# Softmax normalisation in a hybrid attention block: one reciprocal for four heads, normalising as a separate step

## The chip, the cores and the metric

The kernel runs on one core of one Trainium2 chip. The metric is the time of one execution on the device in microseconds (us). Engines: TensorE (PE; its weight loads are shown apart, as PEld), VectorE (DVE), ScalarE (ACT), GpSimd (POOL) and SyncE (SP), whose queue issues the loads from device memory.

## What is computed

One layer of a decoder block over 512 tokens of width 1024, in float32. Cut to what matters here (`masked_softmax` is an ordinary softmax over the allowed keys):

```python
h = rms_norm(x, norm_pre)
proj = h @ w_in                       # 15 pieces: queries, keys, values, gates, ...
kc, vc = compress_blocks(k_c, ...), compress_blocks(v_c, ...)   # flat @ w1, gelu, @ w2
# attention: 8 heads in 2 groups of 4; per head three branches with their own gates g
o = g[..., 0:1] * o_cmp + g[..., 1:2] * o_sel + g[..., 2:3] * o_win
y_a = (o * silu(z_n)) @ w_nsa_o
o_b = retention_sequence(q_r, k_r, v_r)        # chunks of 128 tokens, 4 heads
y_b = (group_norm(o_b) * silu(z_r)) @ w_ret_o
x = x + rms_norm((sigmoid(m_a) * y_a + sigmoid(m_b) * y_b) @ w_out, norm_post)
```

With 512 tokens all 8 key blocks are selected and the window covers the sequence, so the selected and the window branch are both causal softmax attention over all earlier tokens, with different keys and values.

## The kernel before

Every matrix product is done in three passes: each operand is split into a high half that TensorE takes in one pass and the low half that is left (`hi`, `lo`), and the product is hi x hi + lo x hi + hi x lo (`mm3`, lines 237 to 240). The weights stream through four buffers `raw` (512 KB a load, SP's queue, line 324). `cp_any` casts half of a load to `whi`, mostly on ACT (line 197), sometimes on DVE (line 205); `sub_split` makes `wlo` on DVE (line 209). There are nine pairs `whi`/`wlo` of 512 columns, and a new load is issued when a split has used up an old one (`split_lo`, lines 363 to 370).

The main sequence of PE (`main`, line 1202) goes through weight blocks: keys and values (A, C), queries (Q), two hidden layers of the compression (H0, H1: 256 columns wide, so each weight half serves two short products only), then Z, MA0, ZR0, QK0, VR0, ZR1, QK1, VR1, MB0, the two output projections and `w_out`. Each block's results go through PSUM; the banks `bank0` and `bank1` take turns as accumulators (`ACC`), so a block's next column of results can start only when the tail step of the one before last has read its bank.

Attention is woven between the blocks' products. A unit is one query tile t of 128 tokens (t = 3 first), one group of 4 heads, and one branch (t = 2, 3: L = 512 or 384 keys) or both branches together (t = 0, 1); there are 12 units. In a unit `att_head` (lines 787 to 821) runs for each of the four heads j:

- two score products into a bank (lines 793, 794),
- on DVE the masked row minimum of the negated scores, which also writes the negated scores to the probability tile P (line 802; it shows as a custom instruction and a read of its accumulator),
- on ACT exp with the row's sum z (line 809),
- on DVE one reciprocal of z, one column or two (line 811),
- the normalisation with 1/z and the branch's gate: one DVE instruction a branch (line 820), or, where the planner's clocks say that ACT is free sooner (line 813), a product 1/z x gate on DVE and a scaling on ACT (lines 814 to 817).

`att_unit` (line 870) waits for the four heads and starts `att_blocks` for pairs of key tiles: four transposes each on PE (line 831), then `att_half` copies them (ACT, high half; DVE, low half) and multiplies with the values. There are eight probability tiles P (`PR`); the last pair of key tiles by number gives a unit's four back (lines 833 to 835).

Nothing of this is written in the order in which it runs. Each step is a Python generator, and `Order.run` (line 90) is a planner: it holds estimated clocks of PE, ACT, DVE, POOL and the loads, adds an estimated cost for each instruction (lines 65 to 88, 187 to 235), and lets that step go on next whose inputs it holds to be ready, by rank. A step that would be too early (`LAG`, `MARGIN`, `SLACK`) waits. So a change in one step moves the instructions of others. The engines take their instructions in the planned order, and semaphores keep them correct where the estimates are off.

The retention (`tail_qk`, `ret`) shares the engines from block QK0 on; `rtab` is its rotary table, one buffer, loaded again for each tile (`load_rtab`, line 931).

Of the kernel before, what the change touches and what calls it, by code (L numbers as in the profile page):

```python
# [145 lines left out]
def block_kernel(ctx: ExitStack, tc, x, xT, g_pre, ws, small, w2s, norm_post, rope_r, dmask, out):  # L146
# [640 lines left out]
    def att_head(t, g, brs, j, slot):  # L787

        L, nb, h, b0 = P * (t + 1), len(brs), g * 4 + j, brs[0]
        s = yield from PS.get()  # L790
        sv = s[:, 0:nb * L].rearrange("p (b c) -> p b c", b=nb)
        q = qT[t][:, h, :]
        mm(sv, q, kA[:, b0:b0 + nb, g, 0:L], True, False)
        e = mm(sv, q, kB[:, b0:b0 + nb, g, 0:L], False, True)
        yield e, "dve"

        Pj = slot["P"]
        pv = Pj[:, 0:nb * L].rearrange("p (b c) -> p b c", b=nb)
        stat = sp.tile([P, 6], FT, name="stat", tag="stat", bufs=12)
        nm, z, rz = (stat[:, 2 * i:2 * i + 2] for i in range(3))  # L800
        for b in range(nb):
            V.tensor_tensor_reduce(pv[:, b, :], sv[:, b, :], maskp[:, 512 - L:512], 1.0, -NEG, OP.add, OP.min,  # L802
                                   nm[:, b:b + 1])
            od.op("dve", 1.04 * L + 80, e)
        e = od.op("dve", 80)
        PS.put(s, e)
        yield e, "act"
        for b in range(nb):
            e = act(pv[:, b, :], pv[:, b, :], AF.Exp, r=e, bias=nm[:, b:b + 1], scale=-1.0, accum_out=z[:, b:b + 1])
        yield e, "dve"  # L810
        e = recip(rz[:, 0:nb], z[:, 0:nb], e)
        gc = h * 3 + 1 + b0
        if max(od.eng["act"], e) + (0.833 * L + 186) * nb + 190 < max(od.eng["dve"], e) + (0.521 * L + 191) * nb:
            e = tt(rz[:, 0:nb], rz[:, 0:nb], gate[:, t, gc:gc + nb], OP.mult, e)
            yield e, "act"
            for b in range(nb):
                e = act(pv[:, b, :], pv[:, b, :], r=e, scale=rz[:, b:b + 1])
        else:
            for b in range(nb):
                e = ts(pv[:, b, :], pv[:, b, :], rz[:, b:b + 1], gate[:, t, gc + b:gc + b + 1], OP.mult, OP.mult, e)  # L820
        slot["pv"], slot["r"] = pv, e

    def att_blocks(t, g, todo, slots, lastblk):

        r = max(s["r"] for s in slots)
        yield lambda: "po" in avs[t, g]
# [2 lines left out]
        for (br, b, kt), pt in zip(todo, pts):  # L829
            for j in range(4):  # L830
                e = tr(pt[:, j * P:(j + 1) * P], slots[j]["pv"][:, b, kt * P:(kt + 1) * P], ident, r)
            od.spawn(att_half(t, g, br, kt, pt, e), 2)
        if lastblk:
            for s in slots:
                PR.put(s["P"], e)

# [14 lines left out]
    def attention():  # L851
        for t in reversed(range(NT)):
# [7 lines left out]
            for g in range(2):  # L860
                for brs in ([(0, 1)] if t <= 1 else [(0,), (1,)]):
                    slots = []
                    for j in range(4):
                        s = {"P": (yield from PR.get())}
                        slots.append(s)
                        od.spawn(att_head(t, g, brs, j, s), 3)
                        yield
                    od.spawn(att_unit(t, g, brs, slots), 2)

    def att_unit(t, g, brs, slots):  # L870
        yield lambda: all("r" in s for s in slots)
        todo = [(br, b, kt) for b, br in enumerate(brs) for kt in range(t + 1)]
        for i in range(0, len(todo), 2):
            od.spawn(att_blocks(t, g, todo[i:i + 2], slots, i + 2 >= len(todo)), 2)

    def att_out():
        for t, g in ((t, g) for t in reversed(range(NT)) for g in range(2)):
# [52 lines left out]

    def load_rtab(i, r):
        rtr[0] = od.dma(P * 2048, r)
        DMA.dma_start(rtab, rope_r[i // 4, i % 4 * P:(i % 4 + 1) * P, :])

    def tail_qk(hp, t, ps, e):
        yield od.need("q0", "q1", "q2", "q3", "cmp0", "cmp1", *([f"ret{hp - 1}{t}"] if hp else []))
        tv = rtab.rearrange("p (s a c) -> p s a c", s=2, a=4)
        pv = ps.rearrange("p (a r c) -> p a r c", a=4, r=2)
        t1 = yield from NAT.get()
# [457 lines left out]
```

## Time and profile before

| | us |
|---|---|
| median of 3 timed runs | 529.1 (529.02 to 531.55) |
| profiled execution | 532.1, of which span 530.3 |
| PE busy in the span | 519.5 |
| PEld (weight loads) busy | 437.1 |
| DVE busy | 383.2 |
| ACT busy | 253.8 |
| POOL busy | 13.6 |

The profiled execution's own time is 1.8 us longer than its span and 3.0 us above the median. A matmul's shown end is modelled and overlaps the next one's start, so PE can look busy for a short time in which it waits; the weight load in front of a matmul (PEld) starts after the wait, and what ended its idle time names the engine that was late. A row names the line of a helper for many operations (L197 for every ACT instruction, L209 for every two-input DVE operation), so the tiles tell them apart: `whi`, `wlo` are weights, `arena_f<-arena_f,stat` is a probability tile, `arena_r<-bank` the copy of transposed data.

### The profile page before, as it was taken

The numbers are of one execution on the slowest core, as the hardware profiler recorded it, in microseconds if no ns is written. First come the engines' busy times: TensorE is split into PE (matmuls) and PEld (weight loads), VectorE is DVE, ScalarE is ACT, GpSimd is POOL, SyncE is SP. The second block draws the span as 40 slices with busy tenths as digits, with TensorE's granted clock in tenths as the row PEclk, the third lists the DMA queues.
The fourth block names the chain that finished last, engine by engine and source line by source line (L and its number), as shares of the span: only waits on it lengthen the run. The fifth ranks groups of instructions, "written<-read, shape, count | busy, mean of one in ns | idle before, by whom it ended". The sixth has DMA issues, their size and how long they took to land.

```text
span 530.3 us, 7276 instructions
## 1 busy us (share of the span) xinstructions
PE 519.5 (98%) x2616; PEld 437.1 (82%) x2616; DVE 383.2 (72%) x920; ACT 253.8 (48%) x549; POOL 13.6 (3%) x32
## 2 busy tenths in 40 slices
PE   8999999999999999999999999999999999999995
PEld 7898887688888888888788888888888888888885
DVE  6779799988898889998867886786737235345533
ACT  6674577746465673755646253524304224113411
POOL 2000000000000000000010000000000000000000
PEclk9999999999999999999999999999999999999999
DMA  8932025602203014150501442131815043304022
GB/s 324 383 122 80 22 80 185 212 1 65 96 21 105 35 41 138 26 192 3 178 2 41 138 129 70 41 119 41 303 55 158 10 150 122 117 1 158 1 97 102
DMA packets 18131, 55.18 MB, mean 104 GB/s; under 512 B 2096, under 2 KB 3120, under 8 KB 18096
## 3 DMA queue, kind: packets, MB, share of 16 engines
q1 hardware_dynamic: 17808, 54.46, 30.6%
q8 instruction: 20, 0.33, 0.3%
q10 hardware_dynamic: 288, 0.27, 0.1%
q14 instruction: 15, 0.12, 0.1%
HBM read 52.63 MB, written 2.10 MB: 103 GB/s over the span
## 4 chain that ended last, share of the span: by engine, by line
PE 91%; DVE 4%; DMA 2%; issue 1%; ACT 1%; DVEq 0%; POOLq 0%; POOL 0%; ACTq 0%
PE bank L230 85%; PE bank L234 6%; DMA raw<-in_stream_dram 2%; DVE wlo L209 1%; ACT whi L197 1%; DVE arena_f L209 0%; DVE arena_r L209 0%; DVE arena_f L222 0%; DVE arena_f L218 0%; DVE nat L209 0%; DVE arena_r L222 0%; ACT arena_f L197 0%; DVE arena_f L802 0%; ACT arena_r L197 0%; POOLq L1393 0%
## 5 line engine op out<-in xcount | busy, mean ns | idle before, releaser
L197 ACT ACTIVATE whi<-raw 128x512 fp32r<-128x512 f32 x150 | 90.6, 627 | 53.9 <-PE bank L230 42.9
L209 DVE TENSOR_TENSOR wlo<-raw,whi 128x512 fp32r<-128x512 f32 x160 | 103.1, 686 | 6.6 <-ACT whi L197 5.9
L230 PE MATMUL bank<-whi,hTh 128*128 128x512 f32 x256 | 100.6, 409 | 1.6 <-DVE arena_r L222 1.1
L230 PE MATMUL bank<-wlo,hTh 128*128 128x512 f32 x256 | 97.1, 395 | 0.1
L230 PE MATMUL bank<-whi,hTl 128*128 128x512 f32 x256 | 97.1, 395 | 0.0
L230 PE MATMUL bank<-arena_r 128*128 128x256 f32 (+2 forms) x328 | 71.2, 336 | 0.1
L197 ACT ACTIVATE arena_r<-bank 128x512 fp32r<-128x512 f32 (+2 forms) x76 | 42.4, 572 | 48.6 <-PE bank L234 46.4
L230 PE MATMUL bank<-hTh,whi 128*128 128x512 f32 x160 | 64.2, 401 | 0.9 <-ACT whi L197 0.9
L230 PE MATMUL bank<-hTh,wlo 128*128 128x512 f32 x160 | 62.8, 392 | 0.1
L230 PE MATMUL bank<-hTl,whi 128*128 128x512 f32 x160 | 62.5, 391 | 0.0
L230 PE MATMUL bank<-arena_r,whi 128*128 128x512 f32 x192 | 59.1, 389 | 0.0
L230 PEld LDWEIGHTS bank<-whi,hTh 128*128 128x128 f32 x256 | 48.6, 190 | 11.0 <-DVE arena_r L222 1.5
L230 PEld LDWEIGHTS bank<-whi,hTl 128*128 128x128 f32 x256 | 48.6, 190 | 10.7
L230 PEld LDWEIGHTS bank<-arena_r 128*128 128x128 f32 x328 | 51.0, 189 | 6.7 <-DVE stat L802 0.4
L230 PEld LDWEIGHTS bank<-wlo,hTh 128*128 128x128 f32 x256 | 48.8, 191 | 9.0 <-DVE wlo L209 0.5
L209 DVE TENSOR_TENSOR arena_r<-bank,arena_r 128x512 fp32r<-128x512 f32 (+2 forms) x68 | 43.9, 655 | 15.6 <-ACT arena_r L197 15.1
L230 PE MATMUL bank<-whi,arena_r 128*128 128x512 f32 (+1 forms) x176 | 48.8, 352 | 0.0
L230 PEld LDWEIGHTS bank<-arena_r,whi 128*128 128x128 f32 x192 | 36.0, 188 | 7.6 <-DVE sg L222 0.2
L197 ACT ACTIVATE arena_f<-arena_f,stat 128x512 f32<-128x512 f32 (+3 forms) x64 | 35.3, 554 | 8.0 <-DVE stat L802 7.9
L230 PE MATMUL bank<-arena_r,wlo 128*128 128x512 f32 x96 | 37.4, 389 | 0.0
L230 PEld LDWEIGHTS bank<-hTh,wlo 128*128 128x128 f32 x160 | 30.0, 188 | 7.5 <-DVE wlo L209 1.0
L230 PEld LDWEIGHTS bank<-whi,arena_r 128*128 128x128 f32 x176 | 32.1, 189 | 4.6
(120 smaller groups left out, 670.1 us busy)
## 6 DMA issues: line engine op xcount, KB each, us to landing
raw<-in_stream_dram SPq DMA_DIRECT2D x79, 512.0 KB, 3.8
arena_f<-in_x_dram SPq DMA_DIRECT2D x8, 512.0 KB, 7.0
arena_f<-in_xT_dram SPq DMA_DIRECT2D x8, 256.0 KB, 6.0
arena_f<-in_rope_r_dram SPq DMA_DIRECT2D x8, 256.0 KB, 2.6
out_dram<-arena_f SPq DMA_DIRECT2D x6, 256.0 KB, 2.0
raw<-in_stream_dram SPq DMA_DIRECT2D x4, 280.0 KB, 7.1
arena_f<-in_norm_post_dram SPq DMA_DIRECT2D x1, 512.0 KB, 8.0
out_dram<-arena_f SPq DMA_DIRECT2D x2, 192.0 KB, 1.9
```

What stands on the lines that cost most here:

```text
L197: S.activation(o, i, func, **kw)
L209: (V if e == "dve" else G).tensor_tensor(o, a, b, op=op)
L230: T.matmul(ps, a, b, start=start, stop=stop)
L234: T.transpose(ps, a, idn)
```

## The change

- The statistics of a unit (minimum, sum, reciprocal of each row) lie in one tile `stat` of 3 x 8 columns for all four heads instead of one of 6 columns a head.
- `att_head` ends with the exponential. A new step `att_norm`, one a unit, waits until all four heads have their sums, makes one reciprocal of 4 columns (one branch) or 8 (two), and then normalises the four heads one after the other, each on DVE or on ACT by the same comparison of the planner's clocks as before.
- A unit's probability tiles are given back by whichever pair of key tiles is transposed last (the count `left`), not by the last by number.
- `tail_qk` also waits until the planner has issued the load of its rotary table.

```diff
-        stat = sp.tile([P, 6], FT, name="stat", tag="stat", bufs=12)
-        nm, z, rz = (stat[:, 2 * i:2 * i + 2] for i in range(3))
+        nm, z = ((slot["stat"][:, i, j * nb:(j + 1) * nb]) for i in range(2))
...
             e = act(pv[:, b, :], pv[:, b, :], AF.Exp, r=e, bias=nm[:, b:b + 1], scale=-1.0, accum_out=z[:, b:b + 1])
-        yield e, "dve"
-        e = recip(rz[:, 0:nb], z[:, 0:nb], e)
-        gc = h * 3 + 1 + b0
-        if max(od.eng["act"], e) + (0.833 * L + 186) * nb + 190 < max(od.eng["dve"], e) + (0.521 * L + 191) * nb:
-            e = tt(rz[:, 0:nb], rz[:, 0:nb], gate[:, t, gc:gc + nb], OP.mult, e)
-            yield e, "act"
-            for b in range(nb):
-                e = act(pv[:, b, :], pv[:, b, :], r=e, scale=rz[:, b:b + 1])
-        else:
-            for b in range(nb):
-                e = ts(pv[:, b, :], pv[:, b, :], rz[:, b:b + 1], gate[:, t, gc + b:gc + b + 1], OP.mult, OP.mult, e)
-        slot["pv"], slot["r"] = pv, e
+        slot["pv"], slot["z"] = pv, e
+
+    def att_norm(t, g, brs, slots):
+
+        L, nb, b0 = P * (t + 1), len(brs), brs[0]
+        yield lambda: all("z" in s for s in slots)
+        yield max(s["z"] for s in slots), "dve"
+        z, rz = (slots[0]["stat"][:, i, 0:4 * nb] for i in (1, 2))
+        er = recip(rz, z, max(s["z"] for s in slots))
+        yield er, "dve"
+        for j, slot in enumerate(slots):
+            pv, gc, c = slot["pv"], (g * 4 + j) * 3 + 1 + b0, slice(j * nb, (j + 1) * nb)
+            if max(od.eng["act"], er) + (0.833 * L + 186) * nb + 190 < max(od.eng["dve"], er) + (0.521 * L + 191) * nb:
+                e = tt(rz[:, c], rz[:, c], gate[:, t, gc:gc + nb], OP.mult, er)
+                yield e, "act"
+                for b in range(nb):
+                    e = act(pv[:, b, :], pv[:, b, :], r=e, scale=rz[:, j * nb + b:j * nb + b + 1])
+            else:
+                for b in range(nb):
+                    e = ts(pv[:, b, :], pv[:, b, :], rz[:, j * nb + b:j * nb + b + 1],
+                           gate[:, t, gc + b:gc + b + 1], OP.mult, OP.mult, er)
+            slot["r"] = e
+            yield
...
-        if lastblk:
+        left[0] -= 1
+        if not left[0]:
             for s in slots:
                 PR.put(s["P"], e)
...
+                    stat = sp.tile([P, 3, 8], FT, name="stat", tag="stat", bufs=4)
...
+                    od.spawn(att_norm(t, g, brs, slots), 2)
                     od.spawn(att_unit(t, g, brs, slots), 2)
...
         rtr[0] = od.dma(P * 2048, r)
+        od.flags.add(f"rt{i}")
...
-        yield od.need("q0", "q1", "q2", "q3", "cmp0", "cmp1", *([f"ret{hp - 1}{t}"] if hp else []))
+        yield od.need("q0", "q1", "q2", "q3", "cmp0", "cmp1", f"rt{4 * hp + t}", *([f"ret{hp - 1}{t}"] if hp else []))
```

Since the planner sets the order, the change moves instructions on every engine from the first unit on. On PE the last 810 of some 2000 rows (from block QK1's last columns on) are the same in both programs, and so are the first 250.

DVE, at the first attention units. L802 (L801 in the new file) is the row minimum, `stat` the statistics, L226 the reciprocal, L218 the normalisation. Before:

```order
L802 ISA arena_f_79,stat_739<-bank3_84,maskp_114 128x512
L802 ISA stat_739 128x1
L226 RECIPROCAL stat_734<-stat_734 128x1
L218 TENSOR_SCALAR arena_f_79<-arena_f_79,stat_734,gate_116 128x512
L802 ISA arena_f_79,stat_762<-bank2_83,maskp_114 128x512
L802 ISA stat_762 128x1
L802 ISA arena_f_79,stat_767<-bank3_84,maskp_114 128x512
L802 ISA stat_767 128x1
L226 RECIPROCAL stat_739<-stat_739 128x1
L218 TENSOR_SCALAR arena_f_79<-arena_f_79,stat_739,gate_116 128x512
L226 RECIPROCAL stat_762<-stat_762 128x1
L218 TENSOR_SCALAR arena_f_79<-arena_f_79,stat_762,gate_116 128x512
```

And now, from the fourth head of the first unit (`stat_729`) on, with the next unit's first heads (`stat_730`):

```order
L801 ISA arena_f_79,stat_729<-bank3_84,maskp_114 128x512
L801 ISA stat_729 128x1
L801 ISA arena_f_79,stat_730<-bank2_83,maskp_114 128x512
L801 ISA stat_730 128x1
L226 RECIPROCAL stat_729<-stat_729 128x4
L801 ISA arena_f_79,stat_730<-bank3_84,maskp_114 128x512
L801 ISA stat_730 128x1
L218 TENSOR_SCALAR arena_f_79<-arena_f_79,stat_729,gate_116 128x512 x2
L209 TENSOR_TENSOR stat_729<-stat_729,gate_116 128x1
```

The pairs of reciprocal and normalisation that stood between the heads are now one reciprocal behind the next unit's first head, with two normalisations on DVE behind it and a gate product for one that ACT does.

PE, at the end of H1 and the start of Z (H1 has `whi` as the weights against `arena_r`, Z has `whi` against `hTh`; `bank6<-arena_r` is a product of probabilities and values, `bank2<-arena_r` a pair of score products). Before, with `whi_1054` as Z's first weights:

```order
L230 MATMUL bank1_82<-whi_1041,arena_r_80 128x256
L230 MATMUL bank1_82<-wlo_1042,arena_r_80 128x256
L230 MATMUL bank6_87<-arena_r_80 128x512 x2
L230 MATMUL bank0_81<-hTh_99,whi_1054 128x512
L230 MATMUL bank0_81<-hTl_100,whi_1054 128x512
L230 MATMUL bank0_81<-hTh_99,wlo_1055 128x512
L230 MATMUL bank0_81<-hTh_99,whi_1057 128x512
L230 MATMUL bank0_81<-hTl_100,whi_1057 128x512
L230 MATMUL bank0_81<-hTh_99,wlo_1058 128x512
L234 MATMUL bank4_85<-ident_89,arena_f_79 128x128 x2
```

Now, with `whi_1026` as Z's first weights:

```order
L230 MATMUL bank1_82<-whi_1001,arena_r_80 128x256
L230 MATMUL bank1_82<-wlo_1002,arena_r_80 128x256
L230 MATMUL bank0_81<-hTh_99,whi_1026 128x512
L230 MATMUL bank0_81<-hTl_100,whi_1026 128x512
L230 MATMUL bank0_81<-hTh_99,wlo_1027 128x512
L230 MATMUL bank2_83<-arena_r_80 128x512 x2
L230 MATMUL bank0_81<-hTh_99,whi_1030 128x512
L230 MATMUL bank0_81<-hTl_100,whi_1030 128x512
L230 MATMUL bank0_81<-hTh_99,wlo_1031 128x512
L234 MATMUL bank5_86<-ident_89,arena_f_79 128x128 x4
L234 MATMUL bank4_85<-ident_89,arena_f_79 128x128 x4
L230 MATMUL bank6_87<-arena_r_80 128x512 x2
```

More attention products now stand between Z's first weights, and fewer between those of H0 and H1.

DVE, ahead of the instruction that frees `bank0` for the first column of block ZR1 (L222, from `bank0_81`; it is the low half of retention values). Before:

```order
L209 TENSOR_TENSOR arena_r_80<-bank4_85,arena_r_80 128x512
L209 TENSOR_TENSOR wlo_2590<-raw_2363,whi_2589 128x512
L209 TENSOR_TENSOR wlo_2602<-raw_2363,whi_2601 128x512
L209 TENSOR_TENSOR wlo_2605<-raw_2389,whi_2604 128x512
L209 TENSOR_TENSOR nat3_104<-bank7_88,nat3_104 64x512
L209 TENSOR_TENSOR arena_f_79<-nat3_104,arena_f_79 64x4x128
L209 TENSOR_TENSOR arena_r_80<-arena_f_79,arena_r_80 128x256
L209 TENSOR_TENSOR wlo_2620<-raw_2389,whi_2619 128x512
L222 SCALAR_TENSOR_TENSOR arena_r_80<-bank0_81,rs3_112,arena_r_80 128x512
```

Now (L1057, L1058 and L216 are the statistics of a retention output):

```order
L209 TENSOR_TENSOR arena_r_80<-arena_f_79,arena_r_80 128x256
L209 TENSOR_TENSOR arena_r_80<-bank5_86,arena_r_80 128x4x128
L209 TENSOR_TENSOR wlo_2590<-raw_2340,whi_2589 128x512
L1057 BN_STATS st_2616<-bank3_84 128x6
L1058 BN_AGGR mv_2614<-st_2616 128x2
L1057 BN_STATS st_2619<-bank3_84 128x6
L1058 BN_AGGR mv_2614<-st_2619 128x2
L216 TENSOR_SCALAR rv_2615<-mv_2614 128x2
L222 SCALAR_TENSOR_TENSOR arena_r_80<-bank0_81,rs3_112,arena_r_80 128x512
```

The last attention outputs and four weight splits stood ahead of it before; now retention steps stand there, and attention has ended earlier.

More of the change, by code (lines that the diff above doesn't have):

```diff
@@ L809, in att_head, with att_blocks @@
             e = act(pv[:, b, :], pv[:, b, :], AF.Exp, r=e, bias=nm[:, b:b + 1], scale=-1.0, accum_out=z[:, b:b + 1])
-        yield e, "dve"
-        e = recip(rz[:, 0:nb], z[:, 0:nb], e)
-        gc = h * 3 + 1 + b0
-        if max(od.eng["act"], e) + (0.833 * L + 186) * nb + 190 < max(od.eng["dve"], e) + (0.521 * L + 191) * nb:
-            e = tt(rz[:, 0:nb], rz[:, 0:nb], gate[:, t, gc:gc + nb], OP.mult, e)
-            yield e, "act"
-            for b in range(nb):
-                e = act(pv[:, b, :], pv[:, b, :], r=e, scale=rz[:, b:b + 1])
-        else:
-            for b in range(nb):
-                e = ts(pv[:, b, :], pv[:, b, :], rz[:, b:b + 1], gate[:, t, gc + b:gc + b + 1], OP.mult, OP.mult, e)
-        slot["pv"], slot["r"] = pv, e
-    def att_blocks(t, g, todo, slots, lastblk):
+        slot["pv"], slot["z"] = pv, e
[19 more added lines that the diff above has]
+            yield
+    def att_blocks(t, g, todo, slots, left):
         r = max(s["r"] for s in slots)
@@ L862, in attention @@
                     slots = []
+                    stat = sp.tile([P, 3, 8], FT, name="stat", tag="stat", bufs=4)
                     for j in range(4):
-                        s = {"P": (yield from PR.get())}
+                        s = {"P": (yield from PR.get()), "stat": stat}
                         slots.append(s)
@@ L872, in att_unit @@
         todo = [(br, b, kt) for b, br in enumerate(brs) for kt in range(t + 1)]
+        left = [(len(todo) + 1) // 2]
         for i in range(0, len(todo), 2):
-            od.spawn(att_blocks(t, g, todo[i:i + 2], slots, i + 2 >= len(todo)), 2)
+            od.spawn(att_blocks(t, g, todo[i:i + 2], slots, left), 2)
     def att_out():
```

## The prediction

> **What bounds the kernel now.** I read the page's head first, then the chain that ended last, then the busy time by stage, and last the waits of the two TensorE rows stage by stage.
>
> ```profile
> span 530.3 us, 7276 instructions
> PE 519.5 (98%) x2616; PEld 437.1 (82%) x2616; DVE 383.2 (72%) x920; ACT 253.8 (48%) x549; POOL 13.6 (3%) x32
> PE 91%; DVE 4%; DMA 2%; issue 1%; ACT 1%; DVEq 0%; POOLq 0%; POOL 0%; ACTq 0%
> ```
>
> PE is busy for 98% of the span and makes 91% of the chain. All other engines matter only where they keep PE waiting. The change leaves PE's 2616 instructions as they are, so its own work neither grows nor shrinks, and the whole question is how much PE waits. The stages (columns: stretch, its length, then busy us and instruction count of PE, PEld, DVE, ACT, POOL):
>
> ```profile
> 76.00:93.00 17.00, 15.93 (x108) 13.71 (x106) 15.32 (x34) 13.22 (x29) 0.00 (x0) 1.00 0.58 179
> 93.00:100.00 7.00, 6.30 (x25) 4.34 (x26) 6.43 (x13) 5.53 (x13) 0.00 (x0) 1.00 0.73 242
> 100.00:200.00 100.00, 100.00 (x518) 84.40 (x517) 86.31 (x232) 59.63 (x140) 0.00 (x0) 1.00 0.18 59
> 250.00:270.00 20.00, 18.92 (x98) 15.76 (x97) 15.45 (x32) 11.63 (x22) 0.72 (x1) 1.00 0.36 119
> 320.00:520.00 200.00, 200.00 (x935) 167.16 (x935) 107.82 (x195) 66.05 (x121) 4.18 (x7) 1.00 0.29 95
> ```
>
> The reader should see two things. From 320 us on PE is full and nothing else is near its limit; its weight loads there fill 167.16/200 = 84% of the time, which is what a PE without waits looks like here. From 76 to 100 us, where the two hidden-layer blocks of the compression (H0, H1) and the first column of block Z run with little attention between them, PE loses 1.07 + 0.70 us, while DVE is busy for 15.32 of 17 and 6.43 of 7. The only other hole is at 250 to 270 us.
>
> The Trainium skill ("Perfetto Trace Analysis", Identifying the Most-Contended Engine) warns that matmul busy time is no measure of headroom and points to the weight loads' share instead. By that rule alone 18% (82% busy) would be open; the 84% of the full stretch shows that here only about 2 points are, so the trace disagrees with that size.
>
> A matmul's shown time hides part of a wait, so I take the waits from PEld, the weight loads, which come just before (columns: waiting row, what ended it, us in total, times, longest). In order, from the answers for 76 to 93, 93 to 100, 100 to 200, and 200 to 300 us:
>
> ```profile
> PEld bank L230 <- DVE wlo L209: 0.8, 1, 0.8
> PEld bank L234 <- DVE arena_r L209: 0.5, 2, 0.3
> PEld bank L230 <- DVE stat L802: 0.3, 1, 0.3
> ...
> PEld bank L230 <- ACT whi L197: 1.3, 1, 1.3
> PEld bank L230 <- DVE wlo L209: 1.0, 2, 0.6
> PEld bank L234 <- ACT arena_f L197: 0.5, 1, 0.5
> ...
> PEld bank L230 <- DVE arena_f L222: 0.3, 1, 0.3
> PEld bank L230 <- DVE stat L802: 0.2, 1, 0.2
> ...
> PEld bank L230 <- DVE arena_r L222: 1.5, 1, 1.5
> PEld bank L230 <- DVE wlo L209: 0.5, 1, 0.5
> ```
>
> That is 1.6 us in H0/H1, 2.8 us at the start of Z, 0.5 us in the next 100 us, and 2.0 us later, of which 1.5 us is the first matmul of block ZR1 waiting until DVE has emptied its PSUM bank. Together 6.9 us: the most that this change can win.
>
> **The change: DVE's and ACT's work.** Prices by shape, with the mean of one after the bar and the total:
>
> ```profile
> L226 DVE RECIPROCAL stat<-stat 128x1 f32<-128x1 f32 x32 | 5.0, 156 | 0.9 <-ACT arena_f L197 0.9
> L226 DVE RECIPROCAL stat<-stat 128x2 f32<-128x2 f32 x16 | 2.5, 158 | 0.1
> L226 DVE RECIPROCAL zc<-zc 128x8 f32<-128x8 f32 x4 | 0.8, 204 | 0.1
> L209 DVE TENSOR_TENSOR zc<-zc,gate 128x8 f32<-128x8 f32 x4 | 0.7, 171 | 0.1
> L218 DVE TENSOR_SCALAR arena_f<-arena_f,stat,gate 128x512 f32<-128x512 f32 x16 | 8.7, 547 | 0.6
> L218 DVE TENSOR_SCALAR arena_f<-arena_f,stat,gate 128x384 f32<-128x384 f32 x16 | 7.7, 480 | 0.6
> L218 DVE TENSOR_SCALAR arena_f<-arena_f,stat,gate 128x256 f32<-128x256 f32 x16 | 5.9, 411 | 0.3
> L218 DVE TENSOR_SCALAR arena_f<-arena_f,stat,gate 128x128 f32<-128x128 f32 x16 | 4.8, 344 | 0.3
> L205 DVE CAST whi<-raw 128x512 fp32r<-128x512 f32 x10 | 4.2, 424 | 0.7 <-PE bank L230 0.6
> L197 ACT ACTIVATE arena_f<-arena_f,stat 128x512 f32<-128x512 f32 x16 | 11.5, 719 | 2.1 <-DVE stat L802 2.0
> L197 ACT ACTIVATE whi<-raw 128x512 fp32r<-128x512 f32 x150 | 90.6, 627 | 53.9 <-PE bank L230 42.9 <-DMA raw<-in_stream_dram 8.3 <-ACT whi L197 0.7
> ```
>
> The 48 reciprocals of the heads (7.5 us) become 8 of four and 4 of eight columns. A reciprocal over four columns is not in the trace; it lies between 156 and 204 ns, I take 180 (midway), so 8 x 0.18 + 4 x 0.20 = 2.3 us: 5.2 us less. In the new order DVE normalises 42 probability tiles instead of 64 and ACT 22 (5 of 512 columns, 5 of 384, 6 of 256, 6 of 128): DVE loses 5 x 0.547 + 5 x 0.480 + 6 x 0.411 + 6 x 0.344 = 9.7 us. For these, 16 small products of reciprocal and gate come to DVE, 16 x 0.17 = 2.7 us (by the 128x8 row; at most that, since theirs have one or two columns), and one cast of weights, 0.4 us. DVE: -5.2 - 9.7 + 2.7 + 0.4 = -11.8 us of 383. ACT's plain scaling of a probability tile is not in the trace either: its bounds at 512 columns are the weight cast, 627, and the exponential that also sums, 719; I take the cast, which is nearest in kind. Scaled with DVE's own fall by shape, 22 of them are about 22 x 0.51 = 11 us more, of which 0.6 us goes back for the cast.
>
> None of this lies on the path by itself, since PE is the path. It counts where DVE is behind, and there I compare how much work stands ahead of a waited-for DVE instruction, and of its reader on PE, in the two orders.
>
> **Place 1: H0 and H1.** Up to the low half of H1's last weights, DVE now has 2 row-minimum steps fewer, 10 reciprocals replaced by 2, 6 normalisations instead of 10, 3 low halves of transposed probabilities fewer, but 2 gate products, one cast and four small operations of the compression more. With 0.69 + 0.08 for a minimum step, 0.69 for a low half and 0.23 to 0.29 for a small one:
>
> ```profile
> L802 DVE CUSTOM_DVE_ANT_0 arena_f<-bank,maskp 128x512 f32<-128x512 f32 x16 | 10.7, 686 | 0.1
> L802 DVE DVE_READ_ACCUMULATOR2_ANT stat<- 128x1 f32 x64 | 5.3, 83 | 0.0
> L209 DVE TENSOR_TENSOR arena_r<-bank,arena_r 128x512 fp32r<-128x512 f32 x56 | 37.9, 686 | 14.8 <-ACT arena_r L197 14.5
> L222 DVE SCALAR_TENSOR_TENSOR arena_f<-arena_f 128x128 f32<-128x128 f32 x2 | 0.6, 287 | 0.0
> L218 DVE TENSOR_SCALAR arena_f<-arena_f 128x128 f32<-128x128 f32 x2 | 0.5, 227 | 0.1
> ```
>
> -1.5 - 1.2 - 2.2 - 2.1 + 0.3 + 0.4 + 1.1 = -5.2 us. PE reaches the same weights with 10 wide matmuls (4 of scores, 6 of values) and 8 transposes fewer. Starts of wide matmuls in a row, and eight transposes in the chain that ended last:
>
> ```profile
> 261.47 0.40 PE L230 MATMUL bank<-whi,hTh 128*128 128x512 f32 x1
> 261.70 0.39 PE L230 MATMUL bank<-wlo,hTh 128*128 128x512 f32 x1
> 102.45 0.87 PE bank L234 x8
> 258.26 0.57 PE L230 MATMUL bank<-arena_r 128*128 128x256 f32 x4
> 258.66 0.45 PE L230 MATMUL bank<-whi,hTh 128*128 128x512 f32 x1
> ```
>
> 10 x 0.23 + 8 x 0.11 = 3.2 us sooner. DVE is 5.2 us sooner, PE asks 3.2 us sooner: 2.0 us of relief against 1.6 us of waits. By this count they go.
>
> **Place 2: the start of Z.** Up to the low half of Z's last weights both orders hold the same ten row minima; DVE has -1.2 (reciprocals) - 2.2 + 0.3 + 0.4 + 6 small compression steps at 0.25 = -1.2 us, and PE has 2 wide matmuls, 8 transposes and about 0.4 us of narrow products more, +1.7 us. That is 2.9 us of relief in all against 1.6 + 2.8 = 4.4 us of waits up to there; 1.5 us stays. It may be less, since the first wait here (1.3 us) is for a load that DVE's splits let go; it may be all 2.8 us, since ACT, 18.75 of 24 us busy in the two stretches, gets about four of the scalings here (2.5 us). I take -2.9.
>
> **Place 3: the bank before ZR1.** Ahead of the DVE instruction that frees it stand all 64 heads in both orders, so the whole -11.8 us; retention steps of chunk 0 and 1 have moved ahead of it and four weight splits behind it, +6.4 us together: DVE is 5.4 us sooner. PE reaches ZR1 with 32 matmuls of 256 columns more (0.10 each by 258.26 to 258.66) and some transposes, 4 us later. 9 us of relief against 1.5 us: this wait goes, and with it half of the 0.5 us before it. I take -1.8; nothing behind it waits (0.2 us after 300).
>
> **What comes instead.** A unit's transposes now need all four exponentials, one reciprocal, and four scalings in place of one after the last exponential. The new order puts other rows between: from the first unit's last score product to its first transpose there are 17 rows of PE before the change and 51 after it. The cover is the main blocks' matmuls; where it is thin, three more scalings at a mean of 0.445 us, on two engines, cost 0.7 us in each of 12 units, 8 us. Below, zero. The 100 us stretch, with attention all through it, has 0.5 us of waits before; I take 1.5 us for the new order, near that end. Two edits cost nothing: the buffers' return moves no instruction of its own, and the rotary-table flag orders steps that already stand in that order. On SP's queue the third rotary-table load now stands ahead of a weight load that preceded it:
>
> ```profile
> raw<-in_stream_dram SPq DMA_DIRECT2D x79, 512.0 KB, 3.8
> ```
>
> The DVE step that this table load waits for stands in DVE's order ahead of the split that lets the weight load go, so nothing is added; were it otherwise, 3.8 us (the landing of a load) would be covered by the nine pairs of weight buffers.
>
> **Sum.** -2.9 - 1.8 + 1.5 = -3.2 us. The profiled execution took 532.1 us, 530.3 of span and 1.8 around it; it is 3.0 us above the median of the three timed runs, 529.1, and would become 528.9. Against the median: 525.9 us. A change under 0.5%, 2.6 us, cannot be told from none here.
>
> **Rivals.** (1) The wait at Z is the weight stream's, not DVE's: a 512 KB load is issued when a split frees a buffer, and the DMA engines are 73% busy from 93 to 100 us, so PE waits as long as before at places 1 and 2 and only place 3 gains: 529.1 - 1.8 = 527.3. For it: the longest single wait there is ended by whi behind a load. Against: the load was released by a DVE split that now comes sooner. The Trainium skill's rule in the section named above, to work on the most-contended engine first, points the same way: DVE at 72% is not that engine. (2) Slower: the joint reciprocal makes PE wait in every unit, at the price of 0.7 us in 12 units, 8 us in place of 1.5: 525.9 + 6.5 = 532.4. It decides from 0.4 us a unit (4.7 us won, over 12). For it: DVE is 86% busy, so a late reciprocal is queued behind splits. Against: the order moved the transposes back. (3) That it does not do what it says is excluded for the instructions: 36 reciprocals are gone from the order; but a changed order can bring a wait where none is now, anywhere from 60 to 310 us, up to a size like place 2's.
>
> **How the numbers follow.** The forecast gets 0.55, its own range 522.8 (nearly all waits gone) to 528.5; rival 1 gets 0.25, rival 2 0.15, the rest of 3 0.05. Range: 522.8 to 531.0, which leaves out most of rival 2. Faster by over 0.5% (below 526.5): 0.45 of the forecast's 0.55 and 0.03 of rival 1, 0.48. Slower (above 531.7): 0.12 of rival 2 and 0.04 of the rest, 0.16. The remainder, 0.36, is no change.
>
> **What would show it.** Right: DVE near 371 us busy, ACT near 264; PEld's waits on wlo and whi between 70 and 100 us about a third of 4.4 us; no wait on the bank at ZR1; from block VR1 on the same times between rows. Wrong: PEld L234 waits ended by the scaled probabilities (arena_f) in most units, which is rival 2; or an unchanged wait for whi behind a load, which is rival 1.

## The result, and the profile after

| | before | after |
|---|---|---|
| median of the runs, us | 529.1 (the first 3 runs); 531.5 (529.02 to 531.59, 6 runs with those 3) | 526.13 (525.85 to 527.69, 7 runs) |
| profiled execution, us | 532.1, span 530.3 | 527.18, span 525.4 |

Run against run, the changed kernel takes 0.9935 of the time of the kernel before, 95% interval 0.9918 to 0.9952. Of 529.4 us (the median of 23 later runs of the kernel before) that is 3.4 us less (2.5 to 4.3). A seventh run of the kernel before, of 2955.66 us, is left out. Its other six lie in two groups, two near 529.1 us and four near 531.5, so the medians alone would put the gain anywhere from 3.0 to 5.4 us; the last section shows where some 2 us of such a spread come from.

The head of the page after, with the shares of the chain that ended last:

```profile
span 525.4 us, 7266 instructions
...
PE 516.6 (98%) x2616; PEld 437.0 (83%) x2616; DVE 370.4 (70%) x879; ACT 263.0 (50%) x570; POOL 13.2 (3%) x32
...
PE 94%; DVE 2%; issue 1%; ACT 1%; DMA 1%; POOLq 0%; DVEq 0%; POOL 0%; ACTq 0%
```

TensorE's instructions are the same 2616. DVE has 12.8 us less to do, ACT 9.2 us more, and DVE's share of the chain fell from 4% to 2%. The busy time by stage, in stretches that hold about the same work as those shown of before (H0 and H1, the start of Z, the next 100 us, the start of ZR1, the end):

```profile
72.00:89.00 17.00, 16.10 (x119) 14.52 (x118) 16.07 (x38) 15.70 (x34) 0.00 (x0) 1.00 0.69 231
89.00:96.00 7.00, 7.00 (x39) 5.82 (x38) 6.85 (x15) 5.93 (x14) 0.00 (x0) 1.00 0.68 231
96.00:200.00 104.00, 104.00 (x543) 88.29 (x542) 87.62 (x238) 68.28 (x163) 0.00 (x0) 1.00 0.16 54
250.00:270.00 20.00, 20.00 (x115) 17.41 (x114) 16.82 (x39) 10.59 (x20) 0.70 (x1) 1.00 0.32 106
320.00:515.00 195.00, 195.00 (x909) 162.98 (x908) 105.06 (x190) 63.78 (x116) 4.09 (x7) 1.00 0.28 95
```

The first number behind the comma is PE's. At the start of Z it is full now (7.00 of 7, before 6.30), and so it is from 250 to 270 us (20.00, before 18.92). H0 and H1 still have a hole of 0.9 us (1.07 before). Yet DVE is as busy as before there (16.07 of 17). The weight loads' waits of 72 to 89, 96 to 200 and 200 to 320 us (from 89 to 96 us there is none):

```profile
PEld bank L230 <- DVE wlo L209: 1.0, 2, 0.7
PEld bank L234 <- DVE arena_r L209: 0.5, 1, 0.5
PEld bank L230 <- DVE arena_r L209: 0.2, 1, 0.2
...
PEld bank L230 <- DVE arena_r L209: 0.2, 1, 0.2
...
PEld bank L230 <- DVE wlo L209: 0.2, 1, 0.2
```

6.9 us of waits have become 2.1. The wait for `whi` at Z is gone, and so is the 1.5 us for the bank ahead of ZR1; H0 and H1 have 1.7 us, as much as before.

Because waits hide in a pipelined engine, I also use a second measure, worked out from the matmuls' starts in the trace. **Lost time** is the time from one block's first matmul to the next block's, less what the matmuls between take at the spacing that they have without waits (0.227 us for one of 512 columns, as in 261.47 to 261.70 above; 0.11 us for a transpose, other smaller ones in proportion). From Q to VR1 it fell from 12.7 to 8.3 us: H0 1.0 to 2.0, H1 2.4 to 0.4, Z 2.9 to 1.5, VR0 up to ZR1 1.6 to 0.5, all others together 4.8 to 4.0. From VR1 to the block `w_out` both kernels keep the same times to 0.1 us. Some 4 us of it are in every kernel.

How far the attention has come by 200 us shows in the windows view, of the row minima alone (64 in all; the number behind x). Before, and after:

```profile
60.00:200.00 140.00, 23.08 (x42) 1.00 0.25 80
```

```profile
60.00:200.00 140.00, 25.84 (x50) 1.00 0.24 80
```

42 of 64 heads before, 50 after: the new order has the attention further ahead. Among the kernels below that number goes with the time better than DVE's load does, with one clear exception (e6).

### The profile page after: what moved, and what is told of

It is laid out like the page before. It is cut to its first block, busy times and chain, and to the rows that moved or that the text cites. A ratio compares the mean times of both kernels' runs of the same rounds, so it can differ in the third digit from the quotient of the medians.

```text
span 525.4 us, 7266 instructions
## 1 busy us (share of the span) xinstructions
PE 516.6 (98%) x2616; PEld 437.0 (83%) x2616; DVE 370.4 (70%) x879; ACT 263.0 (50%) x570; POOL 13.2 (3%) x32
## 4 chain that ended last, share of the span: by engine, by line
PE 94%; DVE 2%; issue 1%; ACT 1%; DMA 1%; POOLq 0%; DVEq 0%; POOL 0%; ACTq 0%
PE bank L230 88%; PE bank L234 6%; DMA raw<-in_stream_dram 1%; ACT arena_f L197 1%; DVE arena_f L218 0%; DVE wlo L209 0%; ACT whi L197 0%; DVE arena_f L222 0%; DVE arena_f L209 0%; DVE arena_r L209 0%; DVE arena_f L801 0%; ACT arena_r L197 0%; POOLq L1408 0%; POOL rr L209 0%; DVEq L1408 0%
## 5 line engine op out<-in xcount | busy, mean ns | idle before, releaser
L230 PE MATMUL bank<-arena_r 128*128 128x256 f32 (+2 forms) x328 | 69.9, 337 | 0.0
L230 PEld LDWEIGHTS bank<-whi,hTl 128*128 128x128 f32 x256 | 48.6, 190 | 10.8
L197 ACT ACTIVATE arena_f<-arena_f,stat 128x512 f32<-128x512 f32 (+3 forms) x86 | 46.2, 551 | 6.8 <-DVE stat L209 3.7
```

The costliest lines, as they stand in the source:

```text
L197: S.activation(o, i, func, **kw)
L230: T.matmul(ps, a, b, start=start, stop=stop)
```

## The experiments

Twelve kernels, each timed in five rounds beside the kernel before on the same chip. Three questions: which part of the change gains; whether it is less work on DVE or another order; whether it is the luck of one order.

**Which part.** The changed kernel with four reciprocals a unit issued again, reckoned by the planner as one, so that the order stays (e1):

```diff
-        er = recip(rz, z, max(s["z"] for s in slots))
+        for j in range(4):
+            V.reciprocal(rz[:, j * nb:(j + 1) * nb], z[:, j * nb:(j + 1) * nb])
+        er = od.op("dve", max(148, 8.3 * 4 * nb + 136), max(s["z"] for s in slots))
```

> The changed kernel's order, kept row for row, but each unit's one reciprocal is issued as four (one a head), which the planner counts as one: 36 reciprocals come back to DVE, about 36 x 0.17 = 6 us. Theory (DVE's work ahead of the weight splits sets PE's waits): the two units ahead of H0 and H1 put 6 of them, 1.0 us, in front of the splits there, which are already late by 1.0 us at H0, so the time goes up by 0.5 to 1.5 us. Rival (the gain comes from the new order alone, whatever DVE does): no change, within 0.3 us.

Measured 527.07 us, ratio 0.995 (0.9932 to 0.9969), beside 0.9935 of the changed kernel: 0.8 us more, which lies in the theory's range, but the intervals overlap, and the lost time is 8.6 us against 8.3. So the joint instruction as such brings 0.2 to 0.3 us by the profile and 0.8 by the timing, which is not told from nothing; this run decides for neither account. DVE's busy time grew by 1.2 us (370.4 to 371.6) and not by the 6 us expected. The reason stands in DVE's timeline of this kernel:

```profile
66.77 0.34 DVE L818 RECIPROCAL stat<-stat 128x1 f32<-128x1 f32 x4
```

Four narrow reciprocals that follow each other take 0.34 us together, not four times 0.15, against 0.17 for the joint one. Putting them together already saved most.

The same four, reckoned as four, which gives a new order with 24 scalings on ACT (e3):

```diff
-        er = recip(rz, z, max(s["z"] for s in slots))
+        for j in range(4):
+            c = slice(j * nb, (j + 1) * nb)
+            er = recip(rz[:, c], z[:, c], max(s["z"] for s in slots))
```

> The changed kernel with the separate step, but four reciprocals a unit, which the planner counts, so that it makes another order. ACT still gets 24 scalings (22 in the changed kernel), so DVE is about 6 us above the changed kernel and 6 us under the one before. Theory (most of DVE's relief is the scalings that the burst of the joint step gives to ACT): at least half of the gain stays, 1.5 to 3 us faster than before. Rival (the joint reciprocal is what counts): no more than 0.5 us faster than before.

Measured 527.3 us, ratio 0.9948 (0.9933 to 0.9963). The separate step without the joint reciprocal has nearly the whole gain. (DVE is busy for 370.8 us here, as in the changed kernel, and not 6 us longer as expected: four reciprocals in a row again.)

The joint reciprocal, but all 64 normalisations on DVE (e4):

```diff
-            if max(od.eng["act"], er) + (0.833 * L + 186) * nb + 190 < max(od.eng["dve"], er) + (0.521 * L + 191) * nb:
+            if False:
```

> The changed kernel, but all 64 normalisations stay on DVE, with the joint reciprocal; the planner makes another order. DVE has about 7 us more than the changed kernel and 5 us less than the one before. Theory (the scalings on ACT are most of it): less than half of the gain is left, 0 to 1.5 us faster than before. Rival (the joint reciprocal is what counts, ACT has its own delays at H0): as fast as the changed kernel, 3 us faster than before.

Measured 528.28 us, ratio 0.9974 (0.996 to 0.9988): less than half of the gain is left without ACT's share.

Both edits, so that only the step itself is new (e12):

> The changed kernel with the separate step, but with four reciprocals a unit, billed as four, and all 64 normalisations on DVE: the work on every engine is that of the kernel before, and only the step is new. Theory (the step pays because ACT takes normalisations in it; DVE's planned load is otherwise as heavy as before): the attention ends later than in the kernel with the joint reciprocal on DVE alone (last row minimum at 239.5 us there), the wait ahead of ZR1 is 1 us or more, and the time is 528.5 to 530.5 us, ratio 0.998 to 1.002. Rival (grouping the four heads in one step is by itself the gain): 526.5 to 528 us, ratio 0.994 to 0.997, as in the kernel with the joint reciprocal on DVE alone or better.

Measured 528.25 us, ratio 0.9971 (0.9952 to 0.9991), with no wait ahead of ZR1. The time lies between the two ranges; the missing wait speaks against the theory. The step gains some 1.5 us (0.5 to 2.5) with no instruction taken off DVE, and adding the joint reciprocal to it (e4) adds nothing. DVE's busy time does fall, from 383.2 to 378.1 us, since four reciprocals or normalisations in a row take less than four times one (four normalisations of 512 columns 1.91 us, a lone one 0.55); e2 below shows that even 7.2 us less in the old order does not move the time. One thing probably makes e12 slower than its order would be: the mean clock granted to TensorE was 0.994 or 0.995 in ten of its twelve executions, where the kernel before never shows less than 0.996. What such a mean means shows in e5 and e6 below.

**Less work, or another order.** The kernel before in its own order without its 48 reciprocals (e2). It leaves out the division: the tiles are scaled with z in place of 1/z.

```diff
-        e = recip(rz[:, 0:nb], z[:, 0:nb], e)
+        e = od.op("dve", max(148, 8.3 * nb + 136), e)
+        rz = z
```

> The kernel before in its own order, but the 48 reciprocals of the heads are left out (a head is scaled by z in place of 1/z); the planner still counts them, so every other row stands where it stood. DVE loses 48 slots of 0.19, 9 us. Theory: ten of them stood ahead of H1's last split, 1.9 us, so that of the 3.4 us lost in H0 and H1 and the 2.9 us in Z about 2 us go, and the 1.6 us before ZR1 goes as well: 2.5 to 4 us faster than before. Rival (the new order, not less work): no change, within 0.5 us.

Measured 529.59 us, ratio 0.9994 (0.998 to 1.0008). DVE has 7.2 us less (376.0 by the page's head), and the time does not move (0.3 us less, -0.4 to 1.1). Since that was too little to be sure, the same with the normalisations left out too (e7):

```diff
-        e = recip(rz[:, 0:nb], z[:, 0:nb], e)
+        e = od.op("dve", max(148, 8.3 * nb + 136), e)
...
-                e = ts(pv[:, b, :], pv[:, b, :], rz[:, b:b + 1], gate[:, t, gc + b:gc + b + 1], OP.mult, OP.mult, e)
+                e = od.op("dve", copy_ns(pv[:, b, :], pv[:, b, :], 2), e, True)
```

> The kernel before in exactly its own order on every engine, but the 48 reciprocals and the 64 normalisations are left out (so the probabilities are not normalised), 36 us of DVE's time in all, more than three times what the change takes off DVE. Theory (the planned order decides): the waits for DVE in H0, H1 and Z go, up to 2.5 us, but the 1.5 us ahead of ZR1 stay, since that bank's release hangs on where TensorE's order has the last attention products; 526.5 to 529 us, ratio 0.995 to 0.999. Rival (DVE's real work decides everywhere): both go, 4 us or more, ratio 0.9925 or less.

Measured 528.5 us, ratio 0.9977 (0.9961 to 0.9992). DVE is down by 30.2 us (383.2 to 353.0), well over twice what the change takes off, and the gain is 1.2 us (0.4 to 2.1). By the trace it comes from H0 and H1. From 76 to 100 us the waits for weights (`whi`, `wlo`), 3.1 us before, are 0.5 us in e7, the one for `whi` at Z included. But at Z, TensorE now waits for ACT's exponentials, which it transposes (0.5 us before; from 76 to 93 us of e7):

```profile
PEld bank L234 <- ACT arena_f L197: 1.6, 1, 1.6
```

By lost time H0 and H1 together fall from 3.4 to some 1.7 us, and Z keeps what it had. So less work on DVE does take away the waits for weights, but in the old order the next wait eats a good part of what is won. Before ZR1 nothing has moved. The chain that ended last, in order of time (start, us, what), of the kernel before:

```profile
252.74 3.20 PE bank L230 x14
...
255.96 0.64 ACT whi L197
...
256.63 0.69 DVE wlo L209
...
257.35 0.70 DVE nat L209
...
258.08 0.69 DVE arena_f L209
...
258.82 0.40 DVE arena_r L209
259.23 0.60 DVE wlo L209
...
259.86 0.76 DVE arena_r L222
...
260.67 3.47 PE bank L230 x14
```

And of the kernel with 30 us less on DVE (e7):

```profile
252.16 0.64 ACT whi L197
...
252.82 0.69 DVE wlo L209
...
253.55 0.71 DVE nat L209
...
254.28 0.69 DVE arena_f L209
...
255.01 0.41 DVE arena_r L209
255.42 0.60 DVE wlo L209
...
256.06 0.76 DVE arena_r L222
...
256.86 3.24 PE bank L230 x13
```

Piece by piece the same, 4.7 us from ACT's cast to PE's restart in both. No queue of old work stands on DVE here: it is a short chain that starts at PE. Its `nat` and `arena_f` are the attention's last sum; from there to the end of the L222 it takes 3.3 us (257.35 to 260.62). In the code of before, the buffers into which this L222 writes are given free only when all of the attention is done (lines 900 to 907: `all(n in od.flags for n in ATT)`). So this wait exists because the last sum starts only 1.8 us before PE would reach ZR1 (260.67 less the wait of 1.5 is 259.2), and it goes when the order ends the attention earlier. How little is enough shows in e12, where DVE runs the same chain row by row and PE does not wait. Its last sum on DVE, and PE's first matmul of ZR1:

```profile
252.87 0.69 DVE L209 TENSOR_TENSOR nat<-bank,nat 64x512 f32<-64x512 f32 x1
...
256.33 0.40 PE L230 MATMUL bank<-whi,hTh 128*128 128x512 f32 x1
```

That is 3.5 us ahead, just more than the chain's 3.3. In the changed kernel, on DVE's timeline, the same last sum and the following instructions that read VR0's banks:

```profile
241.24 0.69 DVE L209 TENSOR_TENSOR nat<-bank,nat 64x512 f32<-64x512 f32 x1 [0.23 <-ACT nat L197]
...
247.91 0.74 DVE L222 SCALAR_TENSOR_TENSOR arena_r<-bank,rs,arena_r 128x512 fp32r<-128x512 f32 x1
...
257.19 0.74 DVE L222 SCALAR_TENSOR_TENSOR arena_r<-bank,rs,arena_r 128x512 fp32r<-128x512 f32 x1
```

The last sum is 16 us earlier, and PE does not wait. The Trainium skill ("Perfetto Trace Analysis", Optimization Strategy) says of a gap to find what blocks it and to make that dependency start sooner or complete faster. The two are told apart here: completing DVE's other work faster (e7) left the 1.5 us; starting the chain sooner took them away.

**ACT's share and the planner's reckoning in the old form.** 22 normalisations forced onto ACT in the kernel before, known to the planner (e5):

```diff
-        if max(od.eng["act"], e) + (0.833 * L + 186) * nb + 190 < max(od.eng["dve"], e) + (0.521 * L + 191) * nb:
+        if j == 3 or j == 1 and g == 0 and t:
```

> The kernel before with one thing altered: 22 of the 64 normalisations are put on ACT (key tile 3 of each unit's four, and some of key tile 1), and the planner is told so; the reciprocal stays one a head. Theory (the planned order decides: with DVE's planned clock freer, the attention work is placed earlier in TensorE's order, and the bank ahead of ZR1 comes free in time): 2 to 3 us less than before, so 526 to 527.5 us, ratio 0.994 to 0.996, and the wait of 1.5 us ahead of ZR1 gone. Rival (the joint reciprocal is what frees DVE): no gain over 0.7 us, ratio 0.9985 to 1.0.

Measured 533.32 us, ratio 1.007 (1.0051 to 1.0089): slower by 3.7 us, with 5.4 us less on DVE. Neither account had it slower. Its wait ahead of ZR1, and right behind it a stretch of its stages (the last three columns are the clock granted to TensorE, the load's share of the DMA engines and GB/s):

```profile
PEld bank L230 <- DVE arena_r L222: 3.8, 1, 3.8
...
260.70:264.10 3.40, 3.40 (x10) 2.61 (x9) 0.99 (x3) 0.42 (x1) 0.00 (x0) 0.50 0.09 24
```

The wait is 2.3 us longer than before. Behind it the granted clock was 0.50 for 3.4 us, and wide matmuls started 0.43 us apart in place of 0.23; that is another 1.7 us (half of 3.4, an estimate). The mean clock of this execution is 0.993; all six have 0.990 or 0.993, so each probably had at least one such stretch. The row minima by 200 us are 42 as before, so the scalings on ACT alone do not bring the attention forward; here its last sum starts later against ZR1 (255.87 us, when PE has already stopped). These 22 are a choice of mine and not the planner's, and another choice might cost less.

The reciprocals issued as before but reckoned at nothing (e6):

```diff
-        e = recip(rz[:, 0:nb], z[:, 0:nb], e)
+        V.reciprocal(rz[:, 0:nb], z[:, 0:nb])
```

> The kernel before with its 48 reciprocals all issued as they were, but the planner reckons them at no time; its rule then chooses ACT for 20 normalisations by itself, and the order is a new one. DVE still does every reciprocal. Theory (the planned order decides): 1.5 to 3 us less than before, ratio 0.994 to 0.997, the wait ahead of ZR1 gone or under 0.5 us. Rival (DVE's real work decides): the reciprocals' 9 us of DVE time are still there and come unplanned, so no gain or a loss of up to 1 us, ratio 0.999 to 1.002.

Measured 530.84 us, ratio 1.0024 (1.0009 to 1.0038). The attention is far ahead (56 row minima by 200 us), and the wait ahead of ZR1 is gone. But over the stretch of 55 to 330 us the weights' low halves are late:

```profile
PEld bank L230 <- DVE wlo L209: 3.3, 5, 1.2
```

And here too the granted clock fell behind these waits, at the start of Z:

```profile
93.40:96.80 3.40, 3.40 (x13) 2.94 (x13) 3.35 (x10) 2.02 (x6) 0.00 (x0) 0.50 0.74 230
```

That costs 1.7 us by the same estimate, more than the 1.3 us that e6 is slower; eight of its twelve executions have the mean clock of this one, 0.995. So an early attention is not enough by itself. That the splits come late because of the work that the planner does not know of is the likely reading; no run isolates it. The theory of the order had this one wrong in sign, and the result lies just past the rival's range.

**The luck of one order.** The planner's constants altered in ways that have nothing to do with the change, in both kernels:

```diff
-MARGIN = 50.0
+MARGIN = 55.0
```

> The kernel before with one planner constant altered that has nothing to do with the change: MARGIN 55 instead of 50. The instructions' number and kind stay, their order on every engine is another. Theory (the change's gain is its own: any order made with less work on DVE and a separate step keeps TensorE waiting less): 528 to 531 us, ratio 0.998 to 1.003. Rival (the gain is the luck of one order): the spread from such an alteration is as large as the gain, so up to 3.5 us either way, and this one may come out as fast as the changed kernel.

> The changed kernel with the same alteration, MARGIN 55 instead of 50; it moves only a few instructions here. Theory (the gain is the change's own): 525.5 to 527.5 us, ratio to the kernel before 0.993 to 0.997. Rival (luck of one order): a few moved instructions can already bring a wait of 1 to 2 us, so 527 to 529 us.

```diff
-SLACK = 700.0
+SLACK = 720.0
```

> The kernel before with another unrelated planner constant altered, SLACK 720 instead of 700, which gives a third order of the same instructions. Theory (the gain is the change's own): 528 to 531 us, ratio 0.998 to 1.003. Rival (luck of one order): anywhere from 525.5 to 533 us, ratio 0.993 to 1.007, overlapping with the changed kernel's.

> The changed kernel with SLACK 720 instead of 700; the order is another on every engine, and 27 normalisations go to ACT in place of 22. Theory (the gain is the change's own): 525.5 to 528 us, ratio 0.993 to 0.998. Rival (luck of one order): anywhere from 525 to 532 us; at or above 529 us the gain would not survive a new order.

Measured: before 530.16 and 529.42 us (ratios 0.9994 and 0.9984, intervals that both hold 1), after 526.02 and 526.7 us (0.9922, interval 0.9899 to 0.9946; 0.9937, interval 0.9913 to 0.9961). The three kernels of each form lie together, and the two groups do not overlap, in their intervals or in any single run (528.24 us and up, 527.69 and down). Of the changed form these are in effect two orders, since MARGIN moves only a few instructions there (e9's lost time and row minima are those of the changed kernel). So far as two or three orders can show it, the gain is no luck of one.

All kernels (row minima done by 200 us; wait for the bank ahead of ZR1; lost time from Q to VR1; all in us but the first and the last):

| kernel | minima | ZR1 | lost | ratio |
|---|---|---|---|---|
| before | 42 | 1.5 | 12.7 | 1 |
| before, MARGIN (e8) | 42 | 1.5 | 11.4 | 0.9994 |
| before, SLACK (e10) | 42 | 1.5 | 10.5 | 0.9984 |
| before, no reciprocals (e2) | 42 | 1.5 | 10.9 | 0.9994 |
| before, no normalising (e7) | 42 | 1.5 | 11.1 | 0.9977 |
| before, 22 on ACT (e5) | 42 | 3.8 | 14.9 | 1.007 |
| before, unreckoned reciprocals (e6) | 56 | 0 | 13.1 | 1.0024 |
| step, four reciprocals, DVE (e12) | 44 | 0 | 9.7 | 0.9971 |
| step, joint reciprocal, DVE (e4) | 48 | 0 | 10.3 | 0.9974 |
| step, four reciprocals, ACT (e3) | 48 | 0 | 8.0 | 0.9948 |
| after, reciprocals back (e1) | 48 | 0 | 8.6 | 0.995 |
| after | 50 | 0 | 8.3 | 0.9935 |
| after, MARGIN (e9) | 50 | 0 | 8.4 | 0.9922 |
| after, SLACK (e11) | 56 | 0 | 8.7 | 0.9937 |

No kernel is clearly ahead of the changed one; its MARGIN variant is level with it within the intervals. The lost time comes from one profiled execution each: the three orders of the kernel before, equal in time, have 10.5 to 12.7 us, so a difference of 2 us in this column decides nothing by itself.

## Why the prediction was right, and which of its steps were not

**The work.** Forecast DVE 371 and ACT 264 us, measured 370.4 and 263.0. The durations that the trace of before did not have, in groups by shape of the profile after:

```profile
L226 DVE RECIPROCAL stat<-stat 128x4 f32<-128x4 f32 x8 | 1.4, 173 | 1.0 <-ACT arena_f L197 0.8
L226 DVE RECIPROCAL stat<-stat 128x8 f32<-128x8 f32 x4 | 0.8, 191 | 1.1 <-ACT arena_f L197 1.1
L209 DVE TENSOR_TENSOR stat<-stat,gate 128x1 f32<-128x1 f32 x10 | 1.5, 151 | 0.0
L209 DVE TENSOR_TENSOR stat<-stat,gate 128x2 f32<-128x2 f32 x6 | 0.9, 147 | 0.0
L197 ACT ACTIVATE arena_f<-arena_f,stat 128x512 f32<-128x512 f32 x21 | 14.8, 716 | 2.5 <-DVE stat L801 2.2 <-DVE stat L209 0.3
```

The reciprocals took 0.173 and 0.191 us (I took 0.18 and 0.20), the gate products 0.15 (0.17). The 5 scalings of 512 columns stand in one group with 16 exponentials: 716 ns on average, where the exponentials alone had 719 before. With 719 for those 16, a scaling took (21 x 716 - 16 x 719) / 5 = 706 ns: near the upper of my two bounds, not the lower one (627) that I took. On ACT that changed nothing.

**Places 1 and 2, -2.9 us.** By the waits 4.4 us became 1.7, -2.7; by lost time H0, H1 and Z together -2.4. The size is right, the place is not: I had place 1 clean and 1.5 us left at place 2; it is the other way round. And the cause is only in part the one named. In the old order 7.2 us less on DVE brought 0.3 us (e2) and 30.2 us less brought 1.2 us (e7), so the 11.8 us that I counted are worth something between these, 0.3 to 1.2 us (an estimate). e7 shows the step that failed: I counted each wait for weights that goes as time won, but behind it PE met the wait for ACT's exponentials (0.5 us, then 1.6). The rest is the order.

**Place 3, -1.8 us.** By the waits -1.8 there and -0.3 ahead of it, by lost time -1.1. The wait went, but the step that I gave for it is wrong: "Ahead of the DVE instruction that frees it stand all 64 heads in both orders, so the whole -11.8 us ... DVE is 5.4 us sooner". That counts DVE as if it had a backlog that reaches back to its first instruction. The groups by line of the kernel before, from 225 to 262 us (behind the second bar DVE's idle time ahead of the group, and who ended it), and from DVE's timeline the largest of these pauses, 4 us ahead of the last sum:

```profile
L209 DVE TENSOR_TENSOR arena_r<-bank,arena_r 128x512 fp32r<-128x512 f32 (+1 forms) x11 | 7.5, 686 | 2.1 <-ACT arena_r L197 1.8
...
253.03 0.69 DVE L209 TENSOR_TENSOR arena_r<-bank,arena_r 128x512 fp32r<-128x512 f32 x1 [1.44 <-ACT arena_r L197]
```

DVE stood idle for 2.1 us there, waiting for copies by ACT, so it had caught up; what is saved earlier is spent in those waits, and e2 and e7 leave the 1.5 us where they were. What takes them away is the earlier end of the attention in the order, which the step alone already does (e12). That the term came out near its size was luck: the wait was 1.5 us in all, and any reason that takes it away gives that number.

**What comes instead, +1.5 us.** It came, in H0 and not spread over the 100 us stretch: lost time there +1.0 us (it is contained in the -2.4 above). The mechanism of rival 2 is seen there once, on DVE's timeline after:

```profile
72.81 0.18 DVE L226 RECIPROCAL stat<-stat 128x4 f32<-128x4 f32 x1 [0.79 <-ACT arena_f L197]
72.90 0.66 DVE L209 TENSOR_TENSOR wlo<-raw,whi 128x512 fp32r<-128x512 f32 x1
```

The joint reciprocal waits 0.79 us for its unit's fourth exponential, and the weight splits that H0 needs are queued behind it on DVE, with three normalisations between them. That this wait is the cause is not shown: e12, whose four reciprocals follow without a pause, loses more at H0 (2.5 us). What both have is the step's normalisations in a row ahead of the splits. The wait at H0 in e12 (its wait rows from 55 to 330 us), and DVE's rows ahead of it:

```profile
PEld bank L230 <- DVE wlo L209: 2.6, 2, 2.1
...
76.89 1.91 DVE L218 TENSOR_SCALAR arena_f<-arena_f,stat,gate 128x512 f32<-128x512 f32 x4
78.72 1.89 DVE L209 TENSOR_TENSOR wlo<-raw,whi 128x512 fp32r<-128x512 f32 x3
```

In all 12 units of the changed kernel together DVE stood idle ahead of the joint reciprocals for 2.1 us (1.0 + 1.1 in the groups above). Behind 96 us PE shows only 0.4 us of waits, so there the wide products cover it.

**The sum.** Forecast -3.2 us, measured -3.4 (2.5 to 4.3). The terms are further off than the sum: places 1 and 2 with what comes instead were forecast at -1.4 and lost time has -2.4 there; place 3 was forecast at -1.8 and has -1.1; another -0.8 is spread over the other blocks. In the two profiled executions the span fell by 4.9 us, of which 0.6 is the start-up before block C, where the instructions are the same. **Rival 1** (the wait at Z is the weight stream's) fell: the wait for `whi` is gone with the load's share of the DMA engines nearly unchanged (0.68, before 0.73), and e7 takes it away in the old order too. The Trainium skill's rule named there ("Perfetto Trace Analysis", Identifying the Most-Contended Engine), to work on that engine first, is borne out for DVE's mere load: e7 shows what 30.2 us less of it are worth. **Rival 2** is seen at most once and does not decide; its sign, L234 waits ended by `arena_f`, is nowhere in the wait rows after. **Rival 3** did not happen here, but e5 shows that it could have: an order with less work on DVE that costs 3.7 us, in part through a lower clock behind its longest wait.

So the forecast was right with a cause that is half wrong, and in part by luck. Some 1.5 us are the separate step (e12; 1.4 with the joint reciprocal, e4), probably more without e12's lower clock. Another 2.1 us come with ACT's share within the step (the changed kernel against e4, whose clock is that of the kernel before); e3 against e12, 1.2 us, says the same but has the clock in it. Whether these 2.1 us are the lighter DVE, which is 5.6 us less busy than in e4, or once more another order is not told apart. The joint reciprocal, the change's first words, gives 0 to 0.8 us, which the runs do not tell from nothing. Why the step lets the attention run ahead is not shown. The order quoted above suggests it (the next unit's row minima, which free the score banks, now stand ahead of the reciprocal), but no run isolates that. How the 2.4 us at H0 to Z split up between less work and order stays open too.

## What to carry to other kernels

Where a planner sets the order, first ask what the change does to the order, and test it with the order held fixed: 30 us off an engine that is 72% busy were worth 1.2 us, a new order of the same instructions 1.5 us. Look at the clock granted in each run before you price a slower one. A wait for an engine is a backlog only if that engine had no idle time before it; otherwise follow the chain to where it starts. And alter an unrelated constant in both kernels: if the two groups of times stay apart, the gain is more than the luck of one order.

## What the runs showed of the hardware

Four reciprocals of one column in a row took 0.34 us and one of four columns 0.17; a lone one took 0.156 in the trace of before. Removing 36 small instructions is worth far less where they follow each other (DVE busy 371.6 with them, 370.4 without).

TensorE's same first instructions, from the first weight block's start to block C, took 24.2, 23.6, 22.6 and 21.9 us in four profiled executions (before, after, e4, e6). This start alone moves a run by some 2 us, as much as the effects sought here. What varies is TensorE's pace. The first matmuls of 512 columns, before and in e6:

```profile
5.66 2.07 PE L230 MATMUL bank<-whi,hTh 128*128 128x512 f32 x4 [0.53 <-ACT whi L197]
...
5.59 1.20 PE L230 MATMUL bank<-whi,hTh 128*128 128x512 f32 x4 [0.65 <-ACT whi L197]
```

In the first three of these executions the matmuls start 0.43 us or more apart at first, and some 0.23 us apart from about 10.8, 9.5 and 7.3 us on; in e6 they do so almost from the first; the traces' record of the full granted clock begins at 10.6, 9.4, 7.2 and 4.6 us. Why it begins at another time in each is not shown.

The granted clock also fell in the middle of two kernels, to 0.50 for 3.4 us: in e5 behind a wait of PE of 3.8 us, in e6 behind two waits of 0.7 and 1.2 us within 2 us. The changed kernel and the kernel before have no such stretch in their profiled executions.

So a single profiled execution is compared stage by stage from Q on, and the times by their intervals.
